# First layer's w_ff1 product in Strassen's form: seven quarter products for eight, with sums of weight quarters on GpSimd

## The chip, the cores and the metric

The kernel runs on one core of one Trainium2 chip. The core has a matrix engine (TensorE, PE in the profile; PEld is its loading of weights), three engines for elementwise work (VectorE or DVE, ScalarE or ACT, GpSimd or POOL), and a queue engine (SyncE or SP) from which all large loads are issued. The metric is device time in microseconds (us) for one execution of the whole program. Less is better.

## The reference

Two layers of a diffusion backbone over 256 latent tokens `x` and 256 context tokens `ctx`, with a model width of 1024 and a hidden width of 4096, all in float32. Each layer has three token mixers and then a gated MLP; a vector `mod`, computed from the condition `c` by the product with `w_mod`, shifts, scales and gates both. What the change touches is the MLP of the first layer, for both token streams:

```python
def modulate(x, g, shift, scale):
    return rms_norm(x, g) * (1 + scale) + shift
def sq_relu_mlp(h, w1, w2):
    return jnp.square(jax.nn.relu(h @ w1)) @ w2
...
        mod = (jax.nn.silu(c) @ w_mod[l] + b_mod[l])[:, None, :]
        mod_c = (jax.nn.silu(c_ctx)[None] @ w_mod[l] + b_mod[l])[:, None, :]
...
        x = x + gt2 * sq_relu_mlp(modulate(x, g_norm2[l], sh2, sc2), w_ff1[l], w_ff2[l])
        if l < DEPTH - 1:
            ctx_s = ctx_s + cgt2 * sq_relu_mlp(modulate(ctx_s, g_norm2[l], csh2, csc2),
                                               w_ff1[l], w_ff2[l])
```

In the first layer (l = 0) both streams go through it, 512 tokens in all; in the second only the latent tokens do.

## The kernel before

Activations lie feature-major: a tile holds 128 features by tokens. Every float32 product is made of three matrix products in the rounded type fp32r: the weights are cut into a high and a low part, and the product is high x high + low x high + high x low. `split` (L379) does the cut for a piece of 128x1024: ACT copies the high part `whi` (L384), DVE subtracts it to get the low part `wlo` (L385). `hilo` does the same for activations (L485, L486). For a few pieces around a norm, `split` puts the subtraction on GpSimd. Weights arrive in raw tiles of 1 MB, of which there are two (pool `rpool`); `wpool` holds four pairs of cut pieces.

The first layer's MLP runs in four blocks b. In each, two sub-blocks q of 512 hidden columns each are multiplied (`fm` on `w_ff1`; 4 chunks of 256 columns a block), relu, square and `hilo` follow, and `project` multiplies the 1024 hidden columns by `w_ff2`, in four chunks of 256 output columns, into the residual `xT` (L491). The first sub-block (b = 0, q = 0) is called hot: it begins as soon as the first stream's normalised input is there, and works in column halves, one stream after the other. All other sub-blocks run matmuls with 512 token columns, 96 of them each, on lines 473, 476 and 478. In the last block `project` works its last two chunks stream by stream, and spreads the next norm (L183, L192, L203, L218, L227, L235) of one stream under the other stream's matmuls; layer 1's first product, named n1L, follows.

Beside this runs a second job, `mods`: the modulation vector of the second half of layer 0 and of layer 1. It is a generator of steps. A step is one DVE operation of 128x512 on a loaded piece of `w_mod` (L349 for the first of a row, L351 for the others); pieces of 512 KB come through two buffers `modr` (L298). After two rows of sums PE adds over partitions and transposes (L308, L318), ACT copies between them (L313), and DVE puts the result into `modT` (L321). `mods.tick()` stands in the loop over contraction tiles in `fm` and takes `mods.rate` steps on average; `mods.drain()` takes all that are left, at the start of the last block's w_ff2 product. Rates come from a table:

```python
RATES = [0.6, 1.3, 0.4, 0.8]
...
        def tick(self):
            self.due += self.rate
            while self.due >= 1:
                self.due -= 1
                next(self.gen, None)
```

The rows of each engine run in a fixed order, which the tile framework sets from the program's order and from when operands and buffers come free. An engine's row waits for its inputs and holds up all rows behind it on that engine. SP's queue works likewise: a load that waits for a buffer holds up the loads behind it. In tile names, the leading part tells the stage (woL0 output projection of layer 0, ffL0 its MLP, n1L1 and convL1 the start of layer 1); `mm`, `mod` and `aux` lie in PSUM, everything else in SBUF.

## Time and profile before

| what | value |
|---|---|
| median of 2 runs | 1148.85 us (1147.17 to 1150.53) |
| the profiled execution | 1148.35 us, span 1146.5 us |
| granted TensorE clock | 0.996 |
| mean load from HBM | 156 GB/s over the span |
| the MLP of layer 0 | from about 393 to about 758 us of the span |

The profiled execution lies half a microsecond from the median. The rows of the profile name a line of the kernel, an engine, an operation and its tiles; their durations are those of this execution. A matmul's row shows the time until its result is out, and successive matmuls overlap, so the price of one in a stream is the distance between starts.

### The profile page before, as it was taken

Reading aid. Unit: us, or ns where it says so; the run is one execution under the profiler, and the core shown is the slowest. Engines: PE = TensorE matmul, PEld = TensorE weight load, DVE = VectorE, ACT = ScalarE, POOL = GpSimd, SP = SyncE. Lnnn points to the kernel's source line nnn. Section 1 sums busy time; section 2 is a strip of 40 time slices with the busy share of each in tenths; the row PEclk is TensorE's granted clock in tenths of the full one; section 3 lists DMA queues with packets and bytes.
Section 4 is the critical chain, followed back from the end, with each engine's and each line's share of the span. In section 5 each row is a group of like instructions: output and inputs, shape, how many; then the busy total and the mean of one; then the engine's idle time right before and its main releaser. Section 6 shows DMA issues by size and latency. Waiting matters only on the chain.

```text
span 1146.5 us, 17789 instructions
## 1 busy us (share of the span) xinstructions
PE 1127.0 (98%) x7075; PEld 983.9 (86%) x7075; DVE 779.6 (68%) x1444; ACT 504.4 (44%) x896; POOL 50.6 (4%) x54
## 2 busy tenths in 40 slices
PE   7899999999999999999999999999999999999998
PEld 6689887887787998878888888899999999988986
DVE  4577775568878876766746664778886567756754
ACT  4345544443332454143134135244666456754752
POOL 0002100000000100000000000043300000000000
PEclk9999999999999999999999999999999999999999
DMA  9933322225655243655456664515434465656653
GB/s 279 295 97 100 107 78 92 82 85 147 202 175 179 91 162 117 196 184 165 146 168 202 217 209 145 199 61 175 139 111 129 131 207 178 184 182 186 184 184 111
DMA packets 156796, 180.03 MB, mean 157 GB/s; under 512 B 5260, under 2 KB 126504, under 8 KB 156712
## 3 DMA queue, kind: packets, MB, share of 16 engines
q1 hardware_dynamic: 156712, 178.88, 50.1%
q8 instruction: 56, 0.92, 0.3%
q14 instruction: 28, 0.23, 0.1%
HBM read 177.81 MB, written 1.05 MB: 156 GB/s over the span
## 4 chain that ended last, share of the span: by engine, by line
PE 88%; DVE 4%; DMA 4%; SPq 2%; ACT 1%; issue 1%; POOL 1%; DVEq 0%; ACTq 0%; POOLq 0%
PE ffL_mm L473 12%; PE ffL_mm L476 12%; PE ffL_mm L478 12%; PE gateL_mm L478 5%; PE gateL_mm L473 5%; PE gateL_mm L476 5%; PE agL_mm L476 3%; PE agL_mm L473 3%; PE agL_mm L478 3%; PE ffL_mm L1112 3%; PE ffL_mm L1111 3%; PE ffL_mm L1110 3%; PE woL_mm L476 2%; PE woL_mm L478 2%; PE woL_mm L473 2%; SPq L105 2%
## 5 line engine op out<-in xcount | busy, mean ns | idle before, releaser
L384 ACT CAST ffL_whi<-ffL_raw 128x1024 fp32r<-128x1024 f32 x128 | 134.4, 1052 | 218.9 <-PE ffL_mm L478 164.3
L385 DVE TENSOR_TENSOR ffL_wlo<-ffL_raw,ffL_whi 128x1024 fp32r<-128x1024 f32 x127 | 155.0, 1222 | 99.3 <-ACT ffL_whi L384 99.1
L473 PE MATMUL ffL_mm<-woL_big,ffL_whi 128*128 128x258 f32 (+2 forms) x544 | 171.0, 329 | 0.0
L476 PE MATMUL ffL_mm<-woL_big,ffL_wlo 128*128 128x258 f32 (+2 forms) x544 | 170.5, 327 | 0.0
L478 PE MATMUL ffL_mm<-woL_big,ffL_whi 128*128 128x258 f32 (+2 forms) x544 | 133.2, 328 | 0.0
L473 PEld LDWEIGHTS ffL_mm<-woL_big,ffL_whi 128*128 128x128 f32 x544 | 103.1, 190 | 10.2 <-issue 1.6
L476 PEld LDWEIGHTS ffL_mm<-woL_big,ffL_wlo 128*128 128x128 f32 x544 | 103.1, 190 | 8.9 <-issue 0.4
L351 DVE SCALAR_TENSOR_TENSOR ffL_acc<-ffL_modr,cs,ffL_acc 128x512 f32<-128x512 f32 x126 | 90.4, 747 | 24.4 <-DMA ffL_modr<-in_w_mod_dram 23.4
L473 PE MATMUL ffL_mm<-ffL_big,ffL_whi 128*128 128x512 f32 (+1 forms) x288 | 105.4, 368 | 0.0
L476 PE MATMUL ffL_mm<-ffL_big,ffL_wlo 128*128 128x512 f32 (+1 forms) x288 | 104.9, 367 | 0.0
L478 PEld LDWEIGHTS ffL_mm<-woL_big,ffL_whi 128*128 128x128 f32 x544 | 91.0, 190 | 8.7
L478 PE MATMUL ffL_mm<-ffL_big,ffL_whi 128*128 128x512 f32 (+1 forms) x288 | 85.1, 367 | 0.0
L473 PEld LDWEIGHTS ffL_mm<-ffL_big,ffL_whi 128*128 128x128 f32 x288 | 54.3, 189 | 10.6 <-issue 2.1
L476 PEld LDWEIGHTS ffL_mm<-ffL_big,ffL_wlo 128*128 128x128 f32 x288 | 54.3, 189 | 9.1 <-issue 0.4
L385 DVE TENSOR_TENSOR gateL_wlo<-gateL_raw,gateL_whi 128x1024 fp32r<-128x1024 f32 x40 | 48.8, 1221 | 19.3 <-ACT gateL_whi L384 19.1
L478 PEld LDWEIGHTS ffL_mm<-ffL_big,ffL_whi 128*128 128x128 f32 x288 | 53.2, 189 | 8.7
L384 ACT CAST gateL_whi<-gateL_raw 128x1024 fp32r<-128x1024 f32 x40 | 42.0, 1051 | 22.0 <-PE gateL_mm L478 18.2
L476 PE MATMUL gateL_mm<-n1L_big,gateL_wlo 128*128 128x512 f32 x128 | 50.7, 396 | 0.0
L473 PE MATMUL gateL_mm<-n1L_big,gateL_whi 128*128 128x512 f32 x128 | 50.5, 396 | 0.0
L1110 PE MATMUL ffL_mm<-ffL_whi,ffL_big 128*128 128x512 f32 x128 | 49.9, 390 | 0.0
L1111 PE MATMUL ffL_mm<-ffL_wlo,ffL_big 128*128 128x512 f32 x128 | 49.8, 389 | 0.0
L1112 PE MATMUL ffL_mm<-ffL_whi,ffL_big 128*128 128x512 f32 x128 | 49.8, 389 | 0.0
(339 smaller groups left out, 2626.8 us busy)
## 6 DMA issues: line engine op xcount, KB each, us to landing
ffL_raw<-in_w_ff_dram SPq DMA_DIRECT2D x64, 1024.0 KB, 5.5
ffL_modr<-in_w_mod_dram SPq DMA_DIRECT2D x53, 512.0 KB, 4.3
gateL_raw<-in_w_in_dram SPq DMA_DIRECT2D x16, 1024.0 KB, 5.3
init_big<-in_w_mod_dram SPq DMA_DIRECT2D x16, 512.0 KB, 7.8
...
agL_modr<-in_w_mod_dram SPq DMA_DIRECT2D x11, 512.0 KB, 5.1
```

The lines of the kernel that those rows point to most:

```text
L105: tc.keep_in_program_order(nc.sync.dma_start(dst, src))
L351: v = V.scalar_tensor_tensor(a, r[:, kk, :], w, a, op0=ALU.mult, op1=ALU.add)
L384: a = A.copy(hi[:, :n], src)
L385: b = eng.tensor_tensor(lo[:, :n], src, hi[:, :n].bitcast(F32), op=ALU.subtract)
L473: m = PE.matmul(d, wh, rh, start=kt == first, stop=False)
L476: PE.matmul(d, wl, rh, start=False, stop=False)
L478: PE.matmul(d, wh, rl, start=False, stop=kt == final)
L1110: PE.matmul(bs[tt], hid[:, 0], wh, start=kk == 0, stop=False)
L1111: PE.matmul(bs[tt], hid[:, 0], wl, start=False, stop=False)
L1112: PE.matmul(bs[tt], hid[:, 1], wh, start=False, stop=kk == nk - 1)
```

## The change

Seven of the eight sub-blocks of layer 0 (all but the hot one) form their product from quarters: the input h is cut by token stream and by half of its features, the weights by half of the features and by alternating 128-column tiles. Seven quarter products (a step each: 24 matmuls of 256 columns) and sums of quarters replace eight. The sums of h are made once, after the hot sub-block (`wino_sums`, 16 DVE operations, four `hilo`), from a plain copy of h that `modulate` now keeps. The sums of weight quarters are made in each sub-block, four of 128x1024 on GpSimd, three of them in place in the raw tiles, which stay held meanwhile. Then the quarters and sums are cut by `parts`. Four of the seven steps accumulate onto a bank that has been copied out by ACT first (`kept`); DVE adds the copies (`added`). Two of the four result quarters are squared on GpSimd, two on ACT. The modulation job runs at rate 0.4 with 14 ticks for each of these sub-blocks, where it had 0.8 with 16. The compute of layer 1 is the same.

```diff
-RATES = [0.6, 1.3, 0.4, 0.8]
+RATES = [0.6, 1.3, 0.4, 0.8, 0.4]
...
-            t = scratch()[:, :S]
+            t = scratch()[:, :S] if keep is None else keep[:, ft, cs]
...
+    def wino_sums(t, sh):
...
+        for k in range(K2):
+            for i, a, b, op0, d, op1 in (
+                (0, q(1, 0, k), c[0][:, k : k + 1], ALU.add, q(1, 1, k), ALU.add),
+                (1, f[:, 0, k], sh[:, k, 0:1], ALU.subtract, q(0, 0, k), ALU.subtract),
+                (2, q(0, 0, k), c[1][:, k : k + 1], ALU.add, q(1, 0, k), ALU.subtract),
+                (3, q(0, 1, k), sh[:, K2 + k, 0:1], ALU.add, f[:, 1, k], ALU.subtract),
+            ):
+                V.scalar_tensor_tensor(f[:, i, k], a, b, d, op0=op0, op1=op1)
+        sa, sb = bigt([P, 4, K2, S]), bigt([P, 4, K2, S])
+        for i in range(4):
+            hilo(sa[:, i], sb[:, i], f[:, i])
+        return sa, sb
+
+    def wino(w, r0, c0, quarters, evict, first):
+        raws = [raw_tile() for _ in range(2)]
...
+        def parts(src):
...
+            A.copy(h, src)
+            V.tensor_tensor(l, src, h.bitcast(F32), op=ALU.subtract)
+            return h, l
+
+        def step(bk, ops, wgt, start=False):
+            ah, al = ops
+            wh, wl = wgt
+            for j in range(2):
+                d = bk[j]
+                for k in range(K2):
+                    for n, (x, y) in enumerate(((wh, ah), (wl, ah), (wh, al))):
+                        PE.matmul(d, x[:, k, j], y[:, k], start=start and k == 0 and n == 0,
+                                  stop=k == K2 - 1 and n == 2, skip_group_check=True)
+                mods.tick()
...
+        p11 = parts(b11)
+        step(ba, quarters["a11"], p11, start=True)
+        m1 = kept(ba)
+        G.tensor_tensor(b11, b12, b11, op=ALU.subtract)
+        step(bb, quarters["s1"], parts(b11), start=True)
+        m5 = kept(bb)
+        G.tensor_tensor(t2, b22, b11, op=ALU.subtract)
+        step(ba, quarters["s2"], parts(t2))
+        u1 = kept(ba)
+        step(bc, quarters["a12"], parts(b21), start=True)
+        added(m1, bc)
+        evict(0, 0, [m1])
+        G.tensor_tensor(b12, b22, b12, op=ALU.subtract)
+        step(ba, quarters["s3"], parts(b12))
+        u2 = kept(ba)
+        V.tensor_tensor(m5, m5, u2, op=ALU.add)
+        evict(1, 1, [m5])
+        step(bb, quarters["s4"], parts(b22))
+        added(u1, bb)
+        evict(0, 1, [u1])
+        G.tensor_tensor(b21, b21, t2, op=ALU.subtract)
+        step(ba, quarters["a22"], parts(b21))
+        evict(1, 0, [x.unsqueeze(1) for x in ba])
...
+                        for i, x in enumerate(src):
+                            A.activation(t[:, i * n : (i + 1) * n], x, AF.Relu)
+                        if r == 0:
+                            G.tensor_tensor(t, t, t, op=ALU.mult)
+                        else:
+                            A.activation(t, t, AF.Square)
...
+                    mods.rate = RATES[4]
+                    wino(w_ff1[l], 0, (b * 2 + q) * per * P, quarters, evict, q == 0)
+                    mods.rate = RATES[3]
+                    continue
...
-    nc = bacc.Bacc("TRN2", target_bir_lowering=False, num_devices=1)
+    nc = bacc.Bacc("TRN2", target_bir_lowering=False, num_devices=1, dynamic_dma_scratch_size=1024)
```

Three places show how the order of rows moves. In the changed kernel's rows, lines behind the inserted code have other numbers: 353 and 351 are the modulation steps (before 351 and 349), 310 and 320 the modulation's matmuls and transposes (308 and 318), 300 its loads (298), 591 the residual (491), 184 the adds of the next norm (183), 204 and 219 its sum over partitions and its broadcast (203 and 218), 541 the matmuls of the new steps, 425 and 475 to 480 the loads and matmuls of `fm` (423 and 473 to 478).

On DVE, at the end of the last w_ff2 product, before: the last modulation steps stand between residuals of that product, and the norm's adds follow.

```order
L351 SCALAR_TENSOR_TENSOR ffL0_acc_1006_6296<-ffL0_modr_1008_6303,cs2_110,ffL0_acc_1006_6296 128x512
L385 TENSOR_TENSOR ffL0_wlo_1049_6561<-ffL0_raw_1035_6474,ffL0_whi_1048_6560 128x1024
L351 SCALAR_TENSOR_TENSOR ffL0_acc_1006_6296<-ffL0_modr_1008_6303,cs2_110,ffL0_acc_1006_6296 128x512
L491 SCALAR_TENSOR_TENSOR xT_131<-ffL0_mm_1036_6476,modT0_132,xT_131 128x256
L491 SCALAR_TENSOR_TENSOR xT_131<-ffL0_mm_1037_6477,modT0_132,xT_131 128x256
L183 TENSOR_TENSOR ffL0_acc_1012_6321<-ffL0_acc_1012_6321,ffL0_scr_1021_6389 128x256
L183 TENSOR_TENSOR ffL0_acc_1012_6321<-ffL0_acc_1012_6321,ffL0_scr_1022_6393 128x256
```

And now, at the same place, right behind the row of the product's last residual:

```order
L323 TENSOR_TENSOR modT1_136<-ffL0_aux_1067_7041,prm1_715 128x4 x2
L351 TENSOR_SCALAR ffL0_acc_1069_7048<-ffL0_modr_1064_7030,cs2_113 128x512
L353 SCALAR_TENSOR_TENSOR ffL0_acc_1069_7048<-ffL0_modr_1064_7030,cs2_113,ffL0_acc_1069_7048 128x512
L353 SCALAR_TENSOR_TENSOR ffL0_acc_1069_7048<-ffL0_modr_1068_7046,cs2_113,ffL0_acc_1069_7048 128x512 x2
L353 SCALAR_TENSOR_TENSOR ffL0_acc_1069_7048<-ffL0_modr_1070_7051,cs2_113,ffL0_acc_1069_7048 128x512 x2
L353 SCALAR_TENSOR_TENSOR ffL0_acc_1069_7048<-ffL0_modr_1071_7055,cs2_113,ffL0_acc_1069_7048 128x512 x2
L351 TENSOR_SCALAR ffL0_acc_1074_7065<-ffL0_modr_1072_7059,cs2_113 128x512
L353 SCALAR_TENSOR_TENSOR ffL0_acc_1074_7065<-ffL0_modr_1072_7059,cs2_113,ffL0_acc_1074_7065 128x512
L353 SCALAR_TENSOR_TENSOR ffL0_acc_1074_7065<-ffL0_modr_1073_7063,cs2_113,ffL0_acc_1074_7065 128x512 x2
L353 SCALAR_TENSOR_TENSOR ffL0_acc_1074_7065<-ffL0_modr_1075_7068,cs2_113,ffL0_acc_1074_7065 128x512 x2
L353 SCALAR_TENSOR_TENSOR ffL0_acc_1074_7065<-ffL0_modr_1076_7072,cs2_113,ffL0_acc_1074_7065 128x512 x2
L184 TENSOR_TENSOR ffL0_acc_1080_7090<-ffL0_acc_1080_7090,ffL0_scr_1089_7158 128x256
```

Three more rows, of six steps, stand between that last residual and the first of these. So the last eleven loads' steps have moved behind the product, and the adds of the next norm behind them.

On PE at that place, before: the last modulation matmul stands among the matmuls of the product's third chunk for one stream.

```order
L478 MATMUL ffL0_mm_1044_6542<-ffL0_big_947_5938,ffL0_whi_1046_6544 128x256
L473 MATMUL ffL0_mm_1044_6542<-ffL0_big_975_6112,ffL0_whi_1048_6560 128x256
L308 MATMUL ffL0_mod_1009_6309<-ffL0_acc_1006_6296,ones_104 32x256 x2
L476 MATMUL ffL0_mm_1044_6542<-ffL0_big_975_6112,ffL0_wlo_1049_6561 128x256
L478 MATMUL ffL0_mm_1044_6542<-ffL0_big_975_6112,ffL0_whi_1048_6560 128x256
L473 MATMUL ffL0_mm_1044_6542<-ffL0_big_975_6112,ffL0_whi_1048_6560 128x256
```

And now:

```order
L478 MATMUL ffL0_mm_1130_7450<-ffL0_big_684_4188,ffL0_wlo_1117_7330 128x256
L480 MATMUL ffL0_mm_1130_7450<-ffL0_big_684_4188,ffL0_whi_1116_7329 128x256
L310 MATMUL ffL0_mod_1065_7034<-ffL0_acc_1056_7002,ones_107 32x256 x2
L310 MATMUL ffL0_mod_1065_7034<-ffL0_acc_1061_7019,ones_107 32x256 x2
L320 MATMUL ffL0_aux_1067_7041<-ident_102,ffL0_scr_1066_7039 128x128 x2
L310 MATMUL ffL0_mod_1077_7078<-ffL0_acc_1069_7048,ones_107 32x256 x2
L310 MATMUL ffL0_mod_1077_7078<-ffL0_acc_1074_7065,ones_107 32x256 x2
L320 MATMUL ffL0_aux_1079_7085<-ident_102,ffL0_scr_1078_7083 128x128 x2
L204 MATMUL ffL0_aux_1120_7376<-ones_107,ffL0_acc_1080_7090 128x1 x2
L204 MATMUL ffL0_aux_1120_7376<-ones_107,ffL0_scr_1119_7374 128x1 x2
L219 MATMUL ffL0_aux_1124_7386<-ffL0_scr_1123_7385,ones_107 128x128 x2
L475 MATMUL n1L1_mm_1151_7561<-ffL0_big_1131_7499,n1L1_whi_1155_7565 128x256
```

The two last sets of modulation matmuls, with the transposes between them, have moved to behind the product's last matmul, and layer 1's first product stands behind both.

On PE in the first sub-block of block 1, before: modulation matmuls among those of the sub-block.

```order
L476 MATMUL ffL0_mm_770_4681<-woL0_big_600_3430,ffL0_wlo_773_4684 128x512
L473 MATMUL ffL0_mm_771_4682<-woL0_big_600_3430,ffL0_whi_772_4683 128x512
L308 MATMUL ffL0_mod_752_4559<-ffL0_acc_728_4375,ones_104 32x256 x2
L308 MATMUL ffL0_mod_752_4559<-ffL0_acc_729_4376,ones_104 32x256 x2
L476 MATMUL ffL0_mm_771_4682<-woL0_big_600_3430,ffL0_wlo_773_4684 128x512
```

And now, between the second step and the third that runs:

```order
L541 MATMUL ffL0_mm_776_4813<-ffL0_big_677_4157,ffL0_wlo_782_4848 128x256
L541 MATMUL ffL0_mm_776_4813<-ffL0_big_678_4158,ffL0_whi_781_4847 128x256
L310 MATMUL ffL0_mod_754_4686<-ffL0_acc_730_4502,ones_107 32x256 x2
L310 MATMUL ffL0_mod_754_4686<-ffL0_acc_731_4503,ones_107 32x256 x2
L320 MATMUL ffL0_aux_763_4745<-ident_102,ffL0_scr_757_4719 128x128 x2
L541 MATMUL ffL0_aux_777_4814<-woL0_big_600_3433,ffL0_whi_787_4912 128x256
```

The transposes, which stood 23 rows behind, now directly follow the modulation matmuls.

On SP, the queue's last modulation loads, before:

```order
L298 DMA ffL0_modr_1005_6294<-in_w_mod_dram 128x2x512
L423 DMA ffL0_raw_1069_6748<-in_w_in_dram 128x8x256
L298 DMA ffL0_modr_1007_6299<-in_w_mod_dram 128x2x512
L298 DMA ffL0_modr_1008_6303<-in_w_mod_dram 128x2x512
L423 DMA ffL0_raw_1070_6750<-in_w_in_dram 128x8x256
L423 DMA convL1_raw_1103_6934<-in_w_in_dram 128x8x256
L664 DMA fouL1_raw_1114_7010<-in_dft_pos_dram 128x2x512
```

And now:

```order
L300 DMA ffL0_modr_1062_7022<-in_w_mod_dram 128x2x512
L425 DMA convL1_raw_1171_7703<-in_w_in_dram 128x8x256
L300 DMA ffL0_modr_1063_7026<-in_w_mod_dram 128x2x512
L764 DMA fouL1_raw_1182_7779<-in_dft_pos_dram 128x2x512
L300 DMA ffL0_modr_1064_7030<-in_w_mod_dram 128x2x512
L766 DMA fouL1_raw_1182_7779<-in_dft_ch_dram 128x256
L300 DMA ffL0_modr_1068_7046<-in_w_mod_dram 128x2x512
L300 DMA ffL0_modr_1070_7051<-in_w_mod_dram 128x2x512
L300 DMA ffL0_modr_1071_7055<-in_w_mod_dram 128x2x512
L300 DMA ffL0_modr_1072_7059<-in_w_mod_dram 128x2x512
L300 DMA ffL0_modr_1073_7063<-in_w_mod_dram 128x2x512
L300 DMA ffL0_modr_1075_7068<-in_w_mod_dram 128x2x512
```

The loads of layer 1's convolution weights and Fourier constants stood behind the last modulation load; now nine modulation loads are queued behind the first of them.

More of the change, by code (lines that the diff above doesn't have):

```diff
@@ L219, in along, with modulate @@
         return rb
-    def modulate(hh, hl, todo, rb, gn, sh):
+    def modulate(hh, hl, todo, rb, gn, sh, keep=None):
         late = []
@@ L482, in fm, with q @@
         return banks
+    K2 = KT // 2
+    def wino_sums(t, sh):
+        f = bigt([P, 4, K2, S], F32)
+        c = [small([P, K2], "wc", bufs=2) for _ in range(2)]
+        V.tensor_tensor(c[0], sh[:, :K2, 1], sh[:, K2:, 1], op=ALU.add)
+        V.tensor_tensor(c[1], sh[:, :K2, 0], sh[:, :K2, 1], op=ALU.subtract)
+        def q(r, kh, k):
+            return t[:, kh * K2 + k, r * S : (r + 1) * S]
+        for k in range(K2):
[10 more added lines that the diff above has]
+        return sa, sb
@@ new lines, in wino, with kept, added @@
+    def wino(w, r0, c0, quarters, evict, first):
+        raws = [raw_tile() for _ in range(2)]
+        for i, r in enumerate(raws):
+            v = w[r0 + i * K2 * P : r0 + (i + 1) * K2 * P, c0 : c0 + 512]
+            nc.sync.dma_start(r.rearrange("p (k n) -> p k n", n=512),
+                              v.rearrange("(k p) n -> p k n", p=P))
+        b = [[r.rearrange("p (k j o n) -> p k j o n", j=2, o=2, n=P)[:, :, :, o] for o in range(2)]
+             for r in raws]
+        t2 = wtmp.tile([P, 1024], F32, tag="t2", name=nm("t2"))
+        t2 = t2.rearrange("p (k j n) -> p k j n", j=2, n=P)
+        (b11, b12), (b21, b22) = b
+        def parts(src):
+            hi = wpool.tile([P, 1024], F32R, tag="whi", name=nm("whi"))
+            lo = wpool.tile([P, 1024], F32R, tag="wlo", name=nm("wlo"))
+            h, l = (x.rearrange("p (k j n) -> p k j n", j=2, n=P) for x in (hi, lo))
+            A.copy(h, src)
[11 more added lines that the diff above has]
+                mods.tick()
+        def kept(bk):
+            t = scratch((P, 2, S))
+            for j in range(2):
+                A.copy(t[:, j], bk[j])
+            return t
+        def added(t, bk):
+            for j in range(2):
+                V.tensor_tensor(t[:, j], t[:, j], bk[j], op=ALU.add)
+        banks = [bank()[:, :S] for _ in range(4)]
+        ba, bb = (banks[:2], banks[2:]) if first else (banks[2:], banks[:2])
+        bc = aux((P, 2, S))
+        bc = [bc[:, j] for j in range(2)]
+        p11 = parts(b11)
[21 more added lines that the diff above has]
+        evict(1, 0, [x.unsqueeze(1) for x in ba])
@@ L983, in hybrid_block_kernel @@
         hh2, hl2 = bigt([P, KT, 512]), bigt([P, KT, 512])
+        if not last:
+            plainh = bigt([P, KT, 512], F32)
         if last:
@@ L1032, in hybrid_block_kernel, with quarter @@
         turns = iter(turn_steps() if last else ())
+        if not last:
+            halves = []
+            def quarter(r, kh):
+                return [h[:, kh * K2 : (kh + 1) * K2, r * S : (r + 1) * S] for h in (hh2, hl2)]
+            quarters = {"a11": quarter(0, 0), "a12": quarter(0, 1), "a22": quarter(1, 1)}
         for b in range(nblk):
@@ L1048, in hybrid_block_kernel @@
                         mods.rate = RATES[3]
+                        if not last and j == 0:
+                            sums = wino_sums(plainh, sh2)
+                            for i in range(4):
+                                quarters[f"s{i + 1}"] = [h[:, i] for h in sums]
+                            halves.append(bigt([P, 2, per, T]))
+                            subs = halves[:]
                     else:
```

21 lines of the change are left out of this document (18 added, 3 removed).

## The prediction

> **What bounds the kernel now.** I read the page first: busy shares, slices, costliest groups, DMA issues.
>
> ```profile
> span 1146.5 us, 17789 instructions
> PE 1127.0 (98%) x7075; PEld 983.9 (86%) x7075; DVE 779.6 (68%) x1444; ACT 504.4 (44%) x896; POOL 50.6 (4%) x54
> PEclk9999999999999999999999999999999999999999
> ...
> L384 ACT CAST ffL_whi<-ffL_raw 128x1024 fp32r<-128x1024 f32 x128 | 134.4, 1052 | 218.9 <-PE ffL_mm L478 164.3
> L385 DVE TENSOR_TENSOR ffL_wlo<-ffL_raw,ffL_whi 128x1024 fp32r<-128x1024 f32 x127 | 155.0, 1222 | 99.3 <-ACT ffL_whi L384 99.1
> L351 DVE SCALAR_TENSOR_TENSOR ffL_acc<-ffL_modr,cs,ffL_acc 128x512 f32<-128x512 f32 x126 | 90.4, 747 | 24.4 <-DMA ffL_modr<-in_w_mod_dram 23.4
> ...
> ffL_modr<-in_w_mod_dram SPq DMA_DIRECT2D x53, 512.0 KB, 4.3
> ```
>
> TensorE (PE) is the bound: busy 98% at full clock. So a matmul saved is time saved, as long as what must be ready for the next one is ready. The profiled run took 1148.35 us with a span of 1146.5; the median shown is 1148.85, so the sum starts from 1148.35, half a microsecond below it. I then read the busy time by stretches: the hot sub-block, the second sub-block of block 0, block 0's w_ff2 product, the last w_ff2 product, and layer 1's first stretch.
>
> ```profile
> 393.00:416.00 23.00, 23.00 (x195) 23.00 (x195) 18.53 (x42) 11.45 (x21) 0.81 (x1) 1.00 0.29 92
> 416.00:437.00 21.00, 21.00 (x103) 17.71 (x102) 15.10 (x19) 14.30 (x23) 0.00 (x0) 1.00 0.70 226
> 437.00:482.00 45.00, 45.00 (x211) 35.99 (x210) 32.13 (x53) 12.13 (x16) 0.00 (x0) 1.00 0.46 141
> 708.00:755.00 47.00, 46.62 (x292) 41.08 (x291) 29.94 (x55) 15.40 (x28) 1.82 (x2) 1.00 0.41 135
> 755.00:800.00 45.00, 41.97 (x343) 41.01 (x342) 40.37 (x76) 23.14 (x44) 18.80 (x12) 1.00 0.42 133
> ```
>
> Columns are length, then busy time of PE, PEld, DVE, ACT, POOL, then clock and DMA. PE never pauses here, DVE is two thirds full and POOL idle: the change hands this stage's work to the two engines whose cover has to last.
>
> **Matmuls: a saving.** Starts of successive matmuls, 512 columns and then 256:
>
> ```profile
> 699.81 0.39 PE L473 MATMUL ffL_mm<-woL_big,ffL_whi 128*128 128x512 f32 x1
> 700.04 0.39 PE L476 MATMUL ffL_mm<-woL_big,ffL_wlo 128*128 128x512 f32 x1
> 700.26 0.39 PE L473 MATMUL ffL_mm<-woL_big,ffL_whi 128*128 128x512 f32 x1
> ...
> 737.97 0.28 PE L473 MATMUL ffL_mm<-ffL_big,ffL_whi 128*128 128x256 f32 x1
> 738.09 0.28 PE L476 MATMUL ffL_mm<-ffL_big,ffL_wlo 128*128 128x256 f32 x1
> ```
>
> One of 512 takes 0.2266 us in a stream (0.225 between these rows), one of 256 takes 0.120, a little over half. A sub-block was 96 of 512 (21.75 us) and becomes 7 steps x 24 of 256 = 168 (20.16 us). Seven sub-blocks change: 7 x 1.59 = 11.1 us less, not an eighth of 152 us. The range of this term is small, the rows are the same instruction.
>
> **Sums, splits and GpSimd: a loss by cover.** Removed per sub-block are 4 splits and about 7 of 13 modulation steps (rate 0.4 on 14 ticks for 0.8 on 16); added are 3 splits, 4 sums of 128x1024 and 2 squares of 128x512 on GpSimd, 8 copies on ACT, 4 adds of 256 columns and one of 512 on DVE. Once, there are 16 sums of 128x256 and 4 hi/lo pairs of 128x1024. What a GpSimd sum does to DVE stands in these rows.
>
> ```profile
> 388.67 2.39 POOL L385 TENSOR_TENSOR ffL_wlo<-ffL_raw,ffL_whi 128x1024 fp32r<-128x1024 f32 x1 [1.54 <-ACT ffL_whi L384]
> 388.94 2.92 DVE L183 TENSOR_TENSOR woL_acc<-woL_acc,woL_scr 128x256 f32<-128x256 f32 x2 [0.51 <-ACT woL_scr L181]
> ...
> 742.18 0.76 DVE L183 TENSOR_TENSOR ffL_acc<-ffL_acc,ffL_scr 128x256 f32<-128x256 f32 x2 [0.67 <-ACT ffL_scr L181]
> ...
> 781.33 2.48 POOL L385 TENSOR_TENSOR convL_wlo<-convL_raw,convL_whi 128x1024 fp32r<-128x1024 f32 x1 [7.35 <-ACT convL_whi L384]
> 781.48 0.41 DVE L637 TENSOR_TENSOR convL_scr<-uL_scr,convL_mm 128x256 f32<-128x256 f32 x1
> 782.00 1.96 DVE L640 TENSOR_SCALAR convL_scr<-convL_scr,prm 128x256 f32<-128x256 f32 x1
> 784.62 0.34 DVE L640 TENSOR_SCALAR convL_scr<-convL_scr,prm 128x256 f32<-128x256 f32 x1
> ```
>
> Two adds that take 0.76 us alone took 2.92 beside a POOL sum and ended with it; a scalar product of 0.34 took 1.96, while L637, with one operand in PSUM, went through in 0.41. So a DVE operation whose operands all lie in SBUF stands still until the POOL sum ends. Four sums at 2.39 and two squares, put at 1.20 each by half the size, block DVE up to 12.0 us in each sub-block.
>
> The Trainium skill, "SBUF — State Buffer" (section on two separate sides), states it more widely: a DVE operation with two SBUF inputs and a GpSimd operation that reads SBUF take one port pair for the whole instruction in turn, "the other fully blocks". The rows above agree for small operations; no row shows a split of 128x1024 waiting. If the rule holds for the splits too, the block is the full 12.0 us, against 4.9 us if the same four sums stood on DVE.
>
> Other DVE rows, the first of which is where the second stream's h begins in the hot sub-block, some 12 us after its first matmul near 393:
>
> ```profile
> 404.78 0.87 DVE L235 SCALAR_TENSOR_TENSOR woL_scr<-xT,woL_gain,woL_aux 128x256 f32<-128x256 f32 x2 [2.48 <-PE woL_aux L218]
> ...
> L491 DVE SCALAR_TENSOR_TENSOR xT<-ffL_mm,modT,xT 128x256 f32<-128x256 f32 x48 | 20.0, 476 | 15.1 <-PE ffL_mm L478 15.1
> L486 DVE TENSOR_TENSOR ffL_big<-ffL_scr,ffL_big 128x512 fp32r<-128x512 f32 x30 | 19.4, 685 | 2.6 <-ACT ffL_big L485 2.6
> ```
>
> I count the DVE rows of the new order from that point to the end of the modulation sums that block 1 waits for (its matmuls of mod stand behind two steps of its first sub-block). Until there PE needs 82 us: 11.5 of the hot sub-block's 23.5, first Strassen sub-block 20.1, w_ff2 product 44.9, two steps 5.8. DVE needs 13 splits and 8 more of w_ff2, 25.7; 37 modulation steps at 0.747, 27.6; 52 operations of 256 columns at about 0.41 (successive starts of L183, L491 and the like), 21.3; four hi/lo of 1024, 4.9; nine of 512, 6.2; some small ones, 2.5. That is 88 us, and up to 19 more under the seven sums and two squares: 107 against 82. DVE also waits at times, as it does now (busy 32 of 45 us in block 0's w_ff2 product), but not every block falls on a row that it stops. The copy of a finished sum (ACT) that these mod matmuls feed stands ahead of the kept quarter products on ACT, so PE's next bank waits too. I take 20 us of PE idle up to there, between 6 without blocking and 25 with all of it, and 6 for the rest of block 1.
>
> In blocks 2 and 3 two sub-blocks follow each other, 40.3 us of PE. Each needs on DVE 7 splits (8.6), adds (2.3), four hi/lo (2.7), 5.6 modulation steps (4.2) and the block (12.0): 29.8, or 60 for the pair. Adds from PSUM run under the block (-3), and the first two splits and the last evictions lie in the w_ff2 products, whose DVE is not full (-9): 47 to 48 against 40, 7 us per block. In all 20 + 6 + 7 + 7 = 40 us. Without any blocking it is 6, and 2 for late first steps; with all of it, and only the PSUM adds taken off the pairs, it is 25 + 3 x 16 = 73. So 8 to 73, and I take 40 because small operations do stop in the rows.
>
> **Modulation vector: a loss on the path.** Seven sub-blocks give up 7.2 steps each, 50 in all, and the drain at the last block then queues them. In the new order 42 modulation steps and some 24 loads of 512 KB stand behind the start of the last w_ff2 product; now:
>
> ```profile
> 710.37 0.39 PE L473 MATMUL ffL_mm<-ffL_big,ffL_whi 128*128 128x512 f32 x1
> ...
> 668.72 12.65 SPq L298 DMA_DIRECT2D ffL_modr<-in_w_mod_dram  x5
> 715.71 9.60 SPq L298 DMA_DIRECT2D ffL_modr<-in_w_mod_dram  x4
> ...
> 735.16 1.54 DVE L351 SCALAR_TENSOR_TENSOR ffL_acc<-ffL_modr,cs,ffL_acc 128x512 f32<-128x512 f32 x2 [3.77 <-DMA ffL_modr<-in_w_mod_dram]
> 739.99 0.74 DVE L351 SCALAR_TENSOR_TENSOR ffL_acc<-ffL_modr,cs,ffL_acc 128x512 f32<-128x512 f32 x1
> ...
> 751.15 0.15 DVE L192 TENSOR_SCALAR ffL_var<-ffL_aux 128x2 f32<-128x2 f32 x1
> 753.88 2.40 POOL L385 TENSOR_TENSOR n1L_wlo<-ffL_raw,n1L_whi 128x1024 fp32r<-128x1024 f32 x1 [1.73 <-issue]
> 754.09 2.99 DVE L183 TENSOR_TENSOR ffL_acc<-ffL_acc,ffL_scr 128x256 f32<-128x256 f32 x2 [0.64 <-ACT ffL_scr L181]
> 758.70 0.28 PE L473 MATMUL n1L_mm<-ffL_big,n1L_whi 128*128 128x256 f32 x1
> 759.80 5.18 POOL L385 TENSOR_TENSOR n1L_wlo<-ffL_raw,n1L_whi 128x1024 fp32r<-128x1024 f32 x2 [3.52 <-ACT n1L_whi L384]
> ```
>
> The last product starts at 710.4 (call it T0); the last modulation step ends at 740.7 (T0+30); layer 1's first product starts at 758.70 (T0+48.3), with PE busy throughout. The load buffers are two, so loads go at 3.1 to 3.2 us each (12.65 over four gaps, 9.60 over three), near (4.3 landing + 1.5 for two steps)/2 = 2.9.
>
> In the new order 20 steps and two scalar products stand behind the last residual of that product, and all squares and adds of the next norm behind them. So this stretch begins when PE has finished the product, T0+46. SP adds to it: the load of the Fourier constants waits there for a raw buffer that GpSimd has to split (three splits, which now begin at T0+43.5 and end at T0+54.6); the last eight modulation loads are queued behind it. I let it begin at T0+50, since DVE's spread no longer holds those splits up: 4.3 to land the first, seven more at 3.0, 1.5 for the last steps: T0+77. Then comes the chain to layer 1: transposes and copy 1.3, nine squares and adds about 4, mean to first matmul 7.55 now (751.15 to 758.70) less 2.2 of POOL block, and 1 for handing over: 12. Start T0+89 instead of T0+48.3: **41 us** in which PE has nothing else, since its order is fixed. Ends: if loads cost nothing, DVE alone needs 16 us behind T0+46 and the chain of some 9, giving T0+70, +22; if all 24 loads run from T0 at 3.2 apart (77, and 6 to land and use the last) with the present 18 us from the last step to layer 1 (740.7 to 758.70), T0+101, +53. I take 41, since the pace is shown in this very stage.
>
> **Sum.** 1148.35 - 11.1 + 40 + 41 = 1218. The parts' ends give 1148.35 - 11.1 + 8 + 22 = 1167 and 1148.35 - 11.1 + 73 + 53 = 1263.
>
> **Rivals.**
> - *Only the drain counts.* POOL and DVE keep up because PE's 20 us per sub-block cover them: 1148.35 - 11.1 + 8 + 41 = 1186. For it: DVE idles a third now, and PSUM operands go through. Against it: 107 us of demand in 82.
> - *The block is not covered at all*, at 73: 1148.35 - 11.1 + 73 + 41 = 1251. For it: GpSimd and DVE write in place what the next step needs, so their waits come in series. Against it: four weight buffers let splits run ahead.
> - *Not slower: modulation catches up.* It decides when 24 loads finish by T0+36, so that the 12 us chain still ends at T0+48: 1.5 us per load instead of 3.1. Then 1148.35 - 11.1 + 8 = 1145. For it: DMA moves 135 GB/s in that stretch, and 226 in an earlier one. Against it: two buffers, and DVE needs 1.5 per load besides its splits. With the drain at its low end (22) and 8 of stalls it is 1167, also within 2%.
> - *The change gives its eighth*: if 256 columns cost half of 512, with all else hidden, 1148.35 - 19 = 1129. Against it: 0.120 is not 0.113.
>
> **How the numbers follow.** A measurement here can tell about 2% (1126 to 1172) from no change. Forecast (1195 to 1245): 0.54. Only the drain: 0.17. Block uncovered: 0.13. Catching up, or the low drain: 0.12, and the eighth: 0.01, all within 2%. Better than 1126: 0.03. Slower 0.84, same 0.13, faster 0.03. The range, 1166 to 1258, leaves out full catching up, the eighth, anything better, and the uppermost part of the uncovered case.
>
> **What would show it.** Matmuls of 256 in the sub-blocks 0.120 apart confirm the first term; 0.113 or less breaks it. DVE splits that take 2 to 3.5 us beside POOL sums, with PE waiting on them, confirm the second; splits at 1.22 throughout and PE busy over 95% from 393 to the last w_ff2 product break it. One idle stretch of PE of about 40 us between the last w_ff2 product and layer 1, released by modulation steps that wait for loads, confirms the third; a gap under 15 us makes my forecast wrong.

## The result, and the profile after

| | before | changed |
|---|---|---|
| median | 1148.85 us (2 runs, 1147.17 to 1150.53) | 1223.01 us (2 runs, 1222.14 to 1223.88) |
| ratio, 95% interval | | 1.0645 (1.0571 to 1.072) |
| span of the profiled execution | 1146.5 us | 1220.3 us |
| mean granted TensorE clock | 0.996 | 0.968 |

The change is slower by 74 us. The page of the changed kernel, busy times first, then the groups that answer to those of before (the modulation steps are now line 353; the splits of the Strassen steps are line 531):

```profile
PE 1134.5 (93%) x7579; PEld 1009.9 (83%) x7579; DVE 883.3 (72%) x1522; ACT 539.7 (44%) x970; POOL 153.9 (13%) x96
PEclk8999999999999999799999999957999999999999
...
L353 DVE SCALAR_TENSOR_TENSOR ffL_acc<-ffL_modr,cs,ffL_acc 128x512 f32<-128x512 f32 x126 | 116.5, 944 | 27.8 <-DMA ffL_modr<-in_w_mod_dram 26.7
L531 DVE TENSOR_TENSOR ffL_wlo<-ffL_raw,ffL_whi 128x1024 fp32r<-128x1024 f32 x42 | 58.5, 1396 | 12.0 <-ACT ffL_whi L530 12.0
```

POOL is three times as busy. The same modulation step takes 944 ns in the mean, where it took 747, and the splits 1396 for 1222. PE fell from 98% to 93%, and its granted clock dips in two places (the 7 and the 57 in the row PEclk). The stretches show where (columns as in the prediction's table): hot sub-block, the first Strassen sub-block, w_ff2 of block 0, then block 1's two sub-blocks in two stretches (with the last 6 us of that product), the last w_ff2 product, and what follows it.

```profile
393.00:422.30 29.30, 22.61 (x182) 21.82 (x180) 26.15 (x47) 10.19 (x19) 8.52 (x4) 0.98 0.27 91
422.30:444.00 21.70, 21.29 (x163) 20.80 (x164) 21.70 (x25) 17.56 (x31) 9.90 (x2) 0.95 0.28 87
444.00:489.00 45.00, 43.94 (x201) 34.01 (x200) 35.18 (x46) 14.43 (x20) 9.61 (x4) 1.00 0.48 158
489.00:534.00 45.00, 31.11 (x209) 28.55 (x208) 35.55 (x50) 10.69 (x19) 9.23 (x4) 0.81 0.40 129
534.00:558.00 24.00, 21.12 (x166) 20.17 (x165) 23.74 (x24) 16.08 (x29) 9.90 (x5) 1.00 0.40 132
...
741.00:789.00 48.00, 48.00 (x312) 42.97 (x311) 34.62 (x53) 13.13 (x19) 3.86 (x3) 1.00 0.64 208
789.00:835.00 46.00, 8.74 (x35) 4.36 (x35) 27.12 (x46) 6.35 (x18) 6.00 (x3) 0.55 0.49 163
```

PE is idle 7 us in the hot stretch, 14 in block 1 and 37 behind the last product. The timeline of that last place, PE's and SP's rows, with the waits in brackets:

```profile
742.52 0.40 PE L475 MATMUL ffL_mm<-ffL_big,ffL_whi 128*128 128x512 f32 x1
...
801.74 17.00 SPq L300 DMA_DIRECT2D ffL_modr<-in_w_mod_dram  x7
...
801.76 1.07 PE L310 MATMUL ffL_mod<-ffL_acc,ones 128*32 128x256 f32 x4 [11.98 <-DVE ffL_acc L353]
...
813.34 1.07 PE L310 MATMUL ffL_mod<-ffL_acc,ones 128*32 128x256 f32 x4 [9.35 <-DVE ffL_acc L353]
...
823.55 1.07 PE L310 MATMUL ffL_mod<-ffL_acc,ones 128*32 128x256 f32 x4 [9.14 <-DVE ffL_acc L353]
...
834.68 0.58 PE L475 MATMUL n1L_mm<-ffL_big,n1L_whi 128*128 128x256 f32 x1 [1.11 <-ACT ffL_big L242]
```

The last product starts at 742.5 (T0) and layer 1's first product at 834.7, 92.2 us behind it, where it was 48.3. The modulation loads go at 2.8 us each (17.00 over six gaps), and PE's modulation matmuls waited 11.98, 9.35 and 9.14 us for the steps.

The whole difference can be laid out. In the profiled executions the MLP starts between 389 and 394.5 us, also where two kernels are the same up to there (394.5 with sums on DVE, 389.1 with idle GpSimd work added, both below); stretches are therefore counted from the first matmul of the hot sub-block (393.5 before, 390.0 after).

| stretch | before | changed | difference |
|---|---|---|---|
| up to the MLP | 393.5 | 390.0 | -3.6 |
| MLP to the start of the last product | 316.8 | 352.5 | +35.7 |
| from there to layer 1's first product | 48.3 | 92.2 | +43.8 |
| layer 1 | 387.8 | 385.6 | -2.2 |
| span | 1146.5 | 1220.3 | +73.8 |

### The profile page after: what moved, and what is told of

Same layout as the page of the kernel before. It is cut to its first block, busy times and chain, and to the rows that moved or that the text cites. A ratio compares the mean times of both kernels' runs of the same rounds, so it can differ in the third digit from the quotient of the medians.

```text
span 1220.3 us, 19027 instructions
## 1 busy us (share of the span) xinstructions
PE 1134.5 (93%) x7579; PEld 1009.9 (83%) x7579; DVE 883.3 (72%) x1522; ACT 539.7 (44%) x970; POOL 153.9 (13%) x96
## 5 line engine op out<-in xcount | busy, mean ns | idle before, releaser
L386 ACT CAST ffL_whi<-ffL_raw 128x1024 fp32r<-128x1024 f32 x100 | 104.7, 1050 | 134.5 <-PE ffL_mm L480 69.1
L387 DVE TENSOR_TENSOR ffL_wlo<-ffL_raw,ffL_whi 128x1024 fp32r<-128x1024 f32 x99 | 120.6, 1221 | 59.9 <-ACT ffL_whi L386 59.7
L353 DVE SCALAR_TENSOR_TENSOR ffL_acc<-ffL_modr,cs,ffL_acc 128x512 f32<-128x512 f32 x126 | 116.5, 944 | 27.8 <-DMA ffL_modr<-in_w_mod_dram 26.7
L541 PE MATMUL ffL_mm<-ffL_big,ffL_whi 128*128 128x256 f32 x448 | 86.2, 288 | 4.7 <-DVE xT L591 4.7
L475 PE MATMUL ffL_mm<-woL_big,ffL_whi 128*128 128x258 f32 (+1 forms) x320 | 83.4, 284 | 0.4 <-DVE xT L591 0.4
L478 PE MATMUL ffL_mm<-woL_big,ffL_wlo 128*128 128x258 f32 (+1 forms) x320 | 83.1, 283 | 0.0
L541 PEld LDWEIGHTS ffL_mm<-ffL_big,ffL_whi 128*128 128x128 f32 x448 | 73.1, 197 | 5.3 <-issue 5.3
L530 ACT CAST ffL_whi<-ffL_raw 128x1024 fp32r<-128x1024 f32 x42 | 44.2, 1055 | 58.4 <-PE ffL_mm L480 36.0
L480 PE MATMUL ffL_mm<-woL_big,ffL_whi 128*128 128x258 f32 (+1 forms) x320 | 63.4, 286 | 6.3 <-DVE woL_big L229 6.3
L541 PE MATMUL ffL_mm<-ffL_big,ffL_wlo 128*128 128x256 f32 x224 | 64.7, 289 | 3.6 <-DVE ffL_wlo L531 3.6
L531 DVE TENSOR_TENSOR ffL_wlo<-ffL_raw,ffL_whi 128x1024 fp32r<-128x1024 f32 x42 | 58.5, 1396 | 12.0 <-ACT ffL_whi L530 12.0
L475 PEld LDWEIGHTS ffL_mm<-ffL_big,ffL_whi 128*128 128x128 f32 x288 | 54.3, 189 | 11.2 <-DVE ffL_scr L553 1.4
L480 PEld LDWEIGHTS ffL_mm<-ffL_big,ffL_whi 128*128 128x128 f32 x288 | 53.0, 189 | 10.3 <-issue 1.6
L475 PEld LDWEIGHTS ffL_mm<-woL_big,ffL_whi 128*128 128x128 f32 x320 | 61.0, 191 | 0.5 <-DVE xT L591 0.5
L478 PEld LDWEIGHTS ffL_mm<-woL_big,ffL_wlo 128*128 128x128 f32 x320 | 61.1, 191 | 0.0
L480 PEld LDWEIGHTS ffL_mm<-woL_big,ffL_whi 128*128 128x128 f32 x320 | 49.2, 193 | 6.7 <-DVE woL_big L229 6.7
```

The lines of the kernel that those rows point to most:

```text
L353: v = V.scalar_tensor_tensor(a, r[:, kk, :], w, a, op0=ALU.mult, op1=ALU.add)
L386: a = A.copy(hi[:, :n], src)
L387: b = eng.tensor_tensor(lo[:, :n], src, hi[:, :n].bitcast(F32), op=ALU.subtract)
L475: m = PE.matmul(d, wh, rh, start=kt == first, stop=False)
L478: PE.matmul(d, wl, rh, start=False, stop=False)
L480: PE.matmul(d, wh, rl, start=False, stop=kt == final)
```

## The experiments

Times are medians where a kernel ran more than once; the kernel before took 1144.6 to 1146.5 us in the median beside them, on the chips of these runs. "Stage" is the stretch from the MLP's first matmul to the first matmul of the last w_ff2 product, "end" from there to layer 1's first product; both are of the profiled execution.

| run | time | ratio to before | stage | end |
|---|---|---|---|---|
| before | 1148.85 | | 316.8 | 48.3 |
| the change | 1223.01 | 1.0645 (1.0571 to 1.072) | 352.5 | 92.2 |
| rate 0.8 | 1200.38 | 1.0476 (1.0455 to 1.0497) | 359.1 | 60.8 |
| sums on DVE | 1205.94 | 1.0526 (1.0505 to 1.0546) | 330.1 | 95.7 |
| before, slow steps | 1193.48 | one run | 318.5 | 92.9 |
| no sums of h | 1216.98 | one run | 345.0 | 92.6 |
| sums on DVE, rate 0.8 | 1168.55 | 1.0187 (1.0158 to 1.0217) | 326.8 | 61.3 |
| sums on DVE, mixed rates | 1166.03 | 1.0164 (1.0134 to 1.0193) | 328.2 | 62.3 |
| sums on DVE, idle GpSimd | 1227.33 | one run | 355.8 | 94.8 |
| from block 1 | 1166.36 | 1.018 (1.0158 to 1.0203) | 327.5 | 60.9 |
| from block 1, mixed rates | 1157.14 | 1.0106 (1.009 to 1.0122) | 330.0 | 48.1 |
| from block 2 | 1146.67 | 0.9997 (0.9981 to 1.0013) | 317.9 | 48.1 |
| three load buffers | 1205.85 | one run | 345.0 | 78.2 |

**The end by itself: the kernel before, with slow steps.**

```diff
+                if not last and (b or q):
+                    mods.rate = 0.35
...
+            if not last:
+                mods.rate = RATES[3]
```

> The kernel before, with its full products, but modulation rate 0.35 in the seven sub-blocks, so that as many steps are deferred as in the change (5.6 per sub-block). Theory (the deferred steps alone make the loss at the end): layer 1's first product starts some 88 to 92 us after the last w_ff2 product's start instead of 48, and little else changes: 1185 to 1200 us. Rival (the late end comes from Strassen's use of raw tiles and GpSimd): below 1165 us.

It came out at 1193.48 us. The stage hardly changed (318.5 for 316.8), and the end is 92.9 us, as in the change (92.2). PE's rows there wait as the changed kernel's do:

```profile
794.43 1.07 PE L308 MATMUL ffL_mod<-ffL_acc,ones 128*32 128x256 f32 x4 [9.28 <-DVE ffL_acc L351]
795.97 0.69 PE L318 MATMUL ffL_aux<-ident,ffL_scr 128*128 128x128 f32 x2 [0.47 <-ACT ffL_scr L313]
799.95 1.02 PE L203 MATMUL ffL_aux<-ones,ffL_acc 128*128 128x1 f32 x4 [3.29 <-DVE ffL_acc L183]
803.27 1.19 PE L218 MATMUL ffL_aux<-ffL_scr,ones 128*128 128x128 f32 x4 [1.44 <-DVE ffL_scr L217]
805.57 0.58 PE L473 MATMUL n1L_mm<-ffL_big,n1L_whi 128*128 128x256 f32 x1 [1.11 <-ACT ffL_big L240]
```

There is no Strassen product and no GpSimd sum in this kernel. The loss at the end is the price of the deferred steps alone.

**The steps earlier: rate 0.8 in the Strassen sub-blocks.**

```diff
-RATES = [0.6, 1.3, 0.4, 0.8, 0.4]
+RATES = [0.6, 1.3, 0.4, 0.8, 0.8]
```

> Rate of the modulation steps in the Strassen sub-blocks 0.8 for 0.4, nothing else. Theory (steps deferred to the end cost the path 44 us there): 39 steps fewer are left, layer 1's first product starts about 48 to 55 us after the last w_ff2 product's start instead of 92, and the extra steps cost some 10 us of PE idle in the sub-blocks, since DVE has 29 us more to do in them: 1185 to 1200 us. Rival (the steps cost the same wherever they stand, because DVE has no room beside the GpSimd sums): the end gains 38 and the sub-blocks lose 29 or more: 1210 to 1220 us.

1200.38 us, 0.4 above the theory's numbers: the end shrinks by 31.4 us, and the stage grows by 6.6, as it now holds more steps. The rival, that they cost the same wherever they stand, fails. The end is still 12 us longer than before.

**What sets the pace of those steps: three load buffers.**

```diff
-                    r = tiny.tile([P, 2, 512], F32, tag="modr", name=nm("modr"), bufs=2)
+                    r = tiny.tile([P, 2, 512], F32, tag="modr", name=nm("modr"), bufs=3)
```

(and the same at the start of the program, where the tag is first used)

> The change as it is, with three buffers for the modulation loads instead of two. Theory (the pace of the deferred steps is set by the turn of two buffers, landing plus two steps, 2.8 us a load): the last eleven loads go at 1.8 to 2.0 us, layer 1's first product starts 80 to 84 us after the last w_ff2 product's start instead of 92: 1209 to 1215 us. Rival (the pace is the bandwidth of the transfers): 1220 to 1225 us.

1205.85 us, below the range: the end is 78.2 us, 14 less, a little better than expected, and the stage is 7.5 us shorter too. DVE's steps waited 6.1 us for loads in the whole span, where they waited 26.7. So the turn of two buffers held these loads up, and not bandwidth alone, though the loads of the end went 2.2 to 2.4 us apart and not at the expected 1.8 to 2.0. A third buffer alone is worth about 17 us here, at the price of 4 KB in each partition.

**GpSimd: the weight sums on DVE, the squares on ACT.**

```diff
-        G.tensor_tensor(b11, b12, b11, op=ALU.subtract)
+        V.tensor_tensor(b11, b12, b11, op=ALU.subtract)
...
-                        if r == 0:
-                            G.tensor_tensor(t, t, t, op=ALU.mult)
-                        else:
-                            A.activation(t, t, AF.Square)
+                        A.activation(t, t, AF.Square)
```

(the three other sums likewise)

> The four weight sums of each sub-block on DVE and all squares on ACT: GpSimd does nothing in the blocks. Theory (GpSimd sums block DVE): DVE gets 4.9 us of sums per sub-block and loses up to 12 us of standing still; splits fall from a mean of 1.40 to 1.22 us and modulation steps from 0.94 to 0.75; the lag at the start of the last w_ff2 product shrinks from 32 to about 15 us: 1203 to 1212 us. Rival (the stalls come from the order of modulation rows and their loads alone): DVE has 34 us more real work, the lag stays or grows: 1220 to 1240 us.

1205.94 us, as the theory had it. DVE has 28 sums more to do, and the stage is 22.4 us shorter (the end is 3.5 us longer). The DVE groups of that stretch (up to the last product), first of the change, then of this kernel:

```profile
L353 DVE SCALAR_TENSOR_TENSOR ffL_acc<-ffL_modr,cs,ffL_acc 128x512 f32<-128x512 f32 x84 | 80.8, 992 | 9.8 <-DMA ffL_modr<-in_w_mod_dram 9.5
...
L586 DVE TENSOR_TENSOR ffL_big<-ffL_scr,ffL_big 128x512 fp32r<-128x512 f32 x29 | 30.2, 1061 | 0.0
...
L575 DVE TENSOR_TENSOR ffL_scr<-ffL_scr,ffL_scr 128x512 f32<-128x512 f32 x7 | 12.7, 1817 | 1.1 <-ACT ffL_scr L548 1.0
```

```profile
L353 DVE SCALAR_TENSOR_TENSOR ffL_acc<-ffL_modr,cs,ffL_acc 128x512 f32<-128x512 f32 x84 | 60.1, 744 | 5.4 <-DMA ffL_modr<-in_w_mod_dram 5.0
L531 DVE TENSOR_TENSOR ffL_wlo<-ffL_raw,ffL_whi 128x1024 fp32r<-128x1024 f32 x42 | 51.2, 1219 | 12.1 <-ACT ffL_whi L530 12.1
...
L586 DVE TENSOR_TENSOR ffL_big<-ffL_scr,ffL_big 128x512 fp32r<-128x512 f32 x30 | 19.8, 685 | 4.5 <-ACT ffL_big L585 4.5
...
L575 DVE TENSOR_TENSOR ffL_scr<-ffL_scr,ffL_scr 128x512 f32<-128x512 f32 x7 | 4.8, 684 | 0.0
```

Without GpSimd at work each operation takes its plain time again. Standing still had cost 84 x 0.248 = 20.8 us on the steps, 42 x 0.177 = 7.4 on the splits, 29 x 0.376 = 10.9 on the activations' low parts (L586), and some 8 on the add of a kept quarter product (L575): 47 us on these four groups. In blocks 2 and 3 PE has no wait left; block 2's pair of sub-blocks, from 597.15 to 638.43, takes 41.28 us of full PE work, where the kernel before needed 44.57 (575.58 to 620.15).

**GpSimd at work for nobody.** To the kernel with sums on DVE, four operations on GpSimd are added in each sub-block, behind a split, into a tile that nothing reads:

```diff
+            if extra:
+                G.tensor_tensor(idle, lo.bitcast(F32), lo.bitcast(F32), op=ALU.subtract)
```

> Sums on DVE as in the run with sums on DVE (rate 0.4), and in each sub-block four GpSimd operations of 128x1024 whose result nobody uses, each behind a split of weights. Theory (a GpSimd operation that reads SBUF stops DVE): the DVE lag returns though nothing waits for GpSimd: mean of the splits and steps rises again, the last w_ff2 product starts 15 to 40 us later than 724.7, total 1220 to 1250 us. Rival (the change lost by waits for GpSimd's results, not by blocking): 1204 to 1210 us as without them.

1227.33 us, 21.4 more than without; the stage is 25.7 us longer. No DVE or ACT row of the stage waits for GpSimd there, so the loss is blocking and not a wait for GpSimd's results. The groups again:

```profile
L353 DVE SCALAR_TENSOR_TENSOR ffL_acc<-ffL_modr,cs,ffL_acc 128x512 f32<-128x512 f32 x84 | 69.8, 859 | 5.5 <-DMA ffL_modr<-in_w_mod_dram 5.4
L533 DVE TENSOR_TENSOR ffL_wlo<-ffL_raw,ffL_whi 128x1024 fp32r<-128x1024 f32 x42 | 59.7, 1421 | 9.2 <-ACT ffL_whi L532 7.5 <-PE ffL_mm L545 1.7
```

Splits are as slow as in the change (1421 ns, there 1396, without GpSimd 1219). Steps are slower than without GpSimd, but not as slow as in the change (859 ns for 744, there 992).

**The sums of h.**

```diff
-                            sums = wino_sums(plainh, sh2)
-                            for i in range(4):
-                                quarters[f"s{i + 1}"] = [h[:, i] for h in sums]
+                            quarters.update(s1=quarter(1, 0), s2=quarter(0, 1), s3=quarter(1, 0), s4=quarter(1, 1))
```

> Leaves out the sums of h and their high and low parts; four steps use other quarters of h instead. Theory (the sums stand between the rows of the second stream's h on DVE and hold up the hot sub-block): PE's two waits there of 2.5 and 3.7 us go, and 1 us of waits at the first Strassen sub-block: 1214 to 1218 us. Rival (these waits come from the GpSimd sum that runs at that time): no change, 1221 to 1224 us.

This kernel leaves out a part of the product, and only its time is of use. It took 1216.98 us, as the theory had it; the stage is 7.5 us shorter, and the two waits in the hot sub-block are gone. The rival was half right, though. These are the rows of the change at that place, POOL, DVE and PE:

```profile
412.54 2.78 POOL L563 TENSOR_TENSOR ffL_raw<-ffL_raw 128x1024 f32<-128x1024 f32 x1 [14.33 <-DVE ffL_wlo L531]
415.40 2.44 POOL L566 TENSOR_TENSOR ffL_t<-ffL_raw,ffL_raw 128x1024 f32<-128x1024 f32 x1
417.80 2.53 POOL L572 TENSOR_TENSOR ffL_raw<-ffL_raw,ffL_raw 128x1024 f32<-128x1024 f32 x1
...
413.04 2.56 DVE L229 SCALAR_TENSOR_TENSOR woL_big<-woL_big,modT,woL_big 128x256 fp32r<-128x256 f32 x1
415.53 2.60 DVE L506 SCALAR_TENSOR_TENSOR ffL_big<-woL_big,ffL_wc 128x256 f32<-128x256 f32 x1
418.05 2.57 DVE L506 SCALAR_TENSOR_TENSOR ffL_big<-ffL_big,modT,woL_big 128x256 f32<-128x256 f32 x1
...
421.06 1.16 PE L480 MATMUL ffL_mm<-woL_big,ffL_whi 128*128 128x256 f32 x4 [3.72 <-DVE woL_big L229]
```

Three sums on GpSimd run one behind the other, and the DVE row that stands in the way of each ends with it, at 2.6 us for 0.48. L229 makes the h that PE waits for. With the sums on DVE one wait of 0.45 us is left of the two in the hot sub-block, though PE then waits 3.49 us in the first Strassen sub-block, where DVE now has these sums to do. So both are needed for the two waits: rows of sums between those of h, and GpSimd that stops them.

**Both undone: sums on DVE and rate 0.8.** The two edits above together.

> Weight sums on DVE, squares on ACT, and rate 0.8 in the Strassen sub-blocks. Theory (two separate losses: GpSimd blocking and deferred steps): both gains add, apart from a few us for DVE, which has 8 us of steps more per pair of sub-blocks (about 44 of 41 us): the last w_ff2 product starts near 722 to 728 us, layer 1's first product 50 to 61 us after it; 1155 to 1175 us. Rival (DVE is simply over-full, so whatever is taken from one place is paid in the other): 1185 to 1205 us.

1168.55 us: the gains do more than add. Together the two edits take 54.5 us off the change's time, alone 22.6 and 17.1. The stage is 32.3 us shorter than at this rate with sums on GpSimd, and the end 34.4 us shorter than with sums on DVE at rate 0.4. So these are two losses, and they bear on each other: the steps put back into the sub-blocks made the stage 6.6 us longer beside GpSimd's sums, and 3.3 us shorter without them. Left are 22.7 us against the kernel before: the end is 13 us longer, and the stage 10 us, though its matmuls are 11.1 us shorter. With rates 1.0 in the products and 0.6 in the sub-blocks:

> As the one before, but rates 1.0 in the w_ff2 products and 0.6 in the Strassen sub-blocks. Theory: the steps lie where DVE has room (31 of 45 us busy in a product), so the pairs of blocks 2 and 3 show no PE wait at all, and the end is the same: 3 to 8 us less than with 0.8 throughout. Rival (the pace of the loads, near 3 us each, limits the products): PE waits move into the products and the time is the same or longer.

1166.03 us; the intervals of the two ratios overlap, so this tells nothing apart in time. PE's waits did leave blocks 2 and 3, but block 1 kept 8 us of them.

**Can the saving be had?** Three kernels use Strassen's form in fewer blocks, with sums on DVE, squares on ACT, and sums of h from their high and low parts, behind block 0's second sub-block. From block 1 on:

```diff
-                if not last and (b or q):
+                if not last and b:
...
+            if not last and b == 0:
+                sums = wino_sums(hh2, hl2)
+                for i in range(4):
+                    quarters[f"s{i + 1}"] = [h[:, i] for h in sums]
```

> Block 0 as before the change; Strassen's form in blocks 1 to 3 only (six sub-blocks), weight sums on DVE, squares on ACT, sums of h formed from its high and low parts behind block 0's second sub-block, rate 0.92, so that as many modulation steps are done as before. Theory (the matmul saving of 1.59 us a sub-block is real and only the three losses hide it): 9.5 us of PE saved, 2 to 10 us lost again where DVE is full (sums of h in block 0's product, 44 of 41 us in the pairs): 1137 to 1147 us, beside 1146 before. Rival (DVE has no room for the extra splits and sums at this rate of steps, and the end stays late by 13 us as in the run with sums on DVE and rate 0.8): 1152 to 1165 us.

> As the one before, with rate 0.9 in the w_ff2 products and 0.8 in the Strassen sub-blocks, the same number of steps in all. Theory (steps belong where DVE has room): 0 to 4 us less than with 0.8 and 0.92. Rival (the pace of the loads binds in the products): the same or more.

1166.36 and 1157.14 us: the first misses the theory by 19 us and lies just above its rival's range. The rival's reason holds in part. In this kernel 24 matmuls of the last product run ahead of the last sub-block's last step, which makes its stage short and its end long in the table; PE waits 3.0 us for DVE at that product's first matmul, and 1.1, 4.3 and 1.1 us behind it. With mixed rates the product starts behind the sub-block, and the end is as before (48.1 us). In both kernels PE waits some 13 us, most of it for DVE, around the start of block 1. DVE has the sums of h to do in block 0's product; that they cause these waits was not tested by itself. Moving steps into the products gains 9 us, more than expected. From block 2 on, with the sums of h spread over four places in blocks 0 and 1:

> Strassen's form in blocks 2 and 3 only (four sub-blocks), weight sums on DVE, squares on ACT; the sums of h in four parts, spread from the end of block 0's first layer product to block 1's; rates 0.85 and 0.8. Theory (with the cover spread, only the matmul saving is left): 4 x 1.59 = 6.4 us saved, 1 to 4 us lost: 1140 to 1144 us beside some 1145 before. Rival (each engine row added to DVE costs the path somewhere): 1148 to 1156 us.

1146.67 us, ratio 0.9997 (0.9981 to 1.0013): no difference, between the theory's range and its rival's. The stage is 317.9 us for 316.8, so 7.5 us were lost beside the 6.4 saved. 3.4 of them are waits of PE that the timeline shows. Some 3.1 are the modulation's matmuls: eight groups of four stand where four groups of eight did, and a group of four held PE as long as one of eight (0.56 and 0.57 us to the next start, and 0.2 more at the matmuls on both sides). The last microsecond was not settled. No version here beats the kernel before.

## Why the prediction was right, point by point

**The matmuls.** 0.120 us a matmul of 256 columns held, and the saving was seen by itself: 44.57 - 41.28 = 3.3 us for a pair of sub-blocks in the kernel with sums on DVE, 3.2 by the prediction.

**Sums, splits and GpSimd: 40 predicted, 46.8 measured** (35.7 net, and 11.1 of matmuls saved). The matmul saving taken off, the blocks compare like this with the kernel before:

| us lost in | block 0 | block 1 | block 2 | block 3 | all |
|---|---|---|---|---|---|
| the change | 15.0 | 19.2 | 4.2 | 8.5 | 46.8 |
| sums on DVE | 15.1 | 10.2 | -0.1 | -0.8 | 24.4 |

Blocking was the right cause of half of it: 22.4 us of the stage go when GpSimd does nothing, although DVE then does the sums, and idle GpSimd operations bring 25.7 back. It is the whole loss of blocks 2 and 3, half of block 1's, and nothing net in block 0. The price of blocking was an upper bound: 12.0 us a sub-block is 84 in all, and the four groups stood still for 47.

The split of the term was off. Blocks 2 and 3 lost 4.2 and 8.5 us where 7 each was predicted, and blocks 0 and 1 lost 34.1 for 26. Some 30 of these lie ahead of the third step of block 1's first sub-block (516.65), where the count of DVE rows gave 20, and 25 at the most. With the sums on DVE it is still some 25, where the count without blocking gave 6, and some 14 with the 8.5 us of seven sums added. So in the first two blocks the count of rows was the weak step: it held only totals, and not which row stood behind which. The hot sub-block alone lost 7.9 us (24.4 us before, from 393.54 to 417.9, and 32.3 now, from 389.98 to 422.27), as rows of h stood behind sums of h. The run without these sums takes 7.4 us off block 0; what makes up the rest of the 24.4 was not separated.

In block 1 the predicted wait for the modulation matmuls came at the predicted place:

```profile
495.20 0.35 PE L541 MATMUL ffL_mm<-woL_big,ffL_whi 128*128 128x256 f32 x1 [1.99 <-DVE xT L591]
...
499.12 4.87 DVE L353 SCALAR_TENSOR_TENSOR ffL_acc<-ffL_modr,cs,ffL_acc 128x512 f32<-128x512 f32 x4
...
499.33 2.79 POOL L580 TENSOR_TENSOR ffL_raw<-ffL_raw,ffL_t 128x1024 f32<-128x1024 f32 x1 [12.77 <-issue]
...
511.98 2.74 DVE L353 SCALAR_TENSOR_TENSOR ffL_acc<-ffL_modr,cs,ffL_acc 128x512 f32<-128x512 f32 x4 [2.41 <-DMA ffL_modr<-in_w_mod_dram]
...
514.11 1.73 PE L310 MATMUL ffL_mod<-ffL_acc,ones 128*32 128x256 f32 x8 [11.43 <-DVE ffL_acc L353]
```

PE waited 11.43 us for steps that were late by DVE's queue, by one GpSimd sum (4.87 us for four steps that take 2.74 in a later row) and by a load (2.41). With the sums on DVE the wait is 6.01, with rate 0.8 it is 5.26, and with both 3.00.

**The modulation vector: 41 predicted, 43.8 measured.** The last step ended at T0+81 (T0+77), the chain from there took 11 us (12), the loads went at 2.8 us (3.0). The kernel before with slow steps shows that this term needs nothing else of the change, and the run with three buffers that the turn of the buffers makes at least 14 us of it.

**The sum: 1218 predicted, 1223 measured.** That it came so near is in part luck. The two terms together were 9.6 us too low, and 5.8 of that came back where nothing was forecast: the MLP started 3.6 us earlier and layer 1 took 2.2 us less.

**The other ways it could have gone.** Only the end counting allowed 8 us for the stage, which lost 46.8; an uncovered block at 73 was too much; the steps did not catch up. What the prediction named as signs came: matmuls at 0.120, splits of up to 3.42 us in the row below, PE idle for 37 us behind the last product: 30.5 us of it in three waits for DVE's steps, the rest in short waits for the adds and small operations behind them.

The splits of the change, as minimum, median and maximum in ns:

```profile
L531 DVE TENSOR_TENSOR ffL_wlo<-ffL_raw,ffL_whi x42: 1206/1212/3419, 411.2 to 732.5; 128x1024 fp32r<-128x1024 f32 x42
```

The median is the plain time: seven of the 42 were stopped. The slowest is this one, which began beside a GpSimd sum that ended at 729.37 and ended 1.08 us behind it:

```profile
726.65 2.72 POOL L580 TENSOR_TENSOR ffL_raw<-ffL_raw,ffL_t 128x1024 f32<-128x1024 f32 x1 [3.50 <-DVE ffL_wlo L531]
...
727.03 3.42 DVE L531 TENSOR_TENSOR ffL_wlo<-ffL_raw,ffL_whi 128x1024 fp32r<-128x1024 f32 x1
```

The Trainium skill, "SBUF — State Buffer" (who interferes with whom), has the loser of the shared ports block for the whole instruction; the prediction left open whether that holds for the large splits. The trace agrees for this split, which took 3.42 us where one takes 1.22 in the mean without GpSimd.
